# A transformer block on one core: columns of the second modulation begin in the last projection round and are spaced differently around the recurrence; the squares of the keys stand ahead of the block copies

## Chip, core, metric

One NeuronCore of a Trainium2 chip runs the whole program in one launch. The metric is device time in microseconds. The engines are named as in the profile: PE (TensorE matmuls), DVE (VectorE), ACT (ScalarE), POOL (GpSimd) and SP, which does nothing here but issue most of the transfers.

## What is computed

For 256 tokens of width 2048, all in fp32:

```python
mod = silu(c) @ w_ada + b_ada                      # 6 * 2048 values: sh1, sc1, gt1, sh2, sc2, gt2
h = rms_norm(x, norm1_g) * (1 + sc1) + sh1
proj = h @ w_in                                    # RWKV, NSA and merge-gate columns
o_a = rwkv7_mix(...)                               # a gated linear recurrence over the tokens
o_b = nsa_mix(...)                                 # compressed, selected and windowed attention
mixed = sigmoid(mg_a) * (o_a @ w_o_rwkv) + sigmoid(mg_b) * (o_b @ w_o_nsa)
x = x + gt1 * (mixed @ w_out)
h = rms_norm(x, norm2_g) * (1 + sc2) + sh2
x = x + gt2 * (square(relu(h @ w_up)) @ w_down)
```

## The kernel before

**Weights.** Every large weight matrix goes through TensorE in two parts, a rounded high part and a rest. One weight step (`weights`, L221) loads 256 rows by up to 512 columns into a buffer of the pool `raw` (4 buffers), ACT rounds it to `whi`, and DVE subtracts to get `wlo` (both pools have 3 buffers). With the activations split the same way, `mm3` does three matmuls for each block, so a usual step is 24 matmuls of 256 columns (`pp`), in the order (hi, hi), (hi weights, low activations), (low weights, hi activations).

**Columns of the modulation.** `mod` isn't computed on TensorE. Of its 96 columns of 128 values each one is a dot product of 128 rows of `w_ada` with silu(c) on DVE. The short form (`ada`, L173) loads a row block in two halves into the same `raw` pool (tile `ar`, 512 KB each), and each half is one DVE instruction (L158) and a small read of the accumulator. Columns 0 to 31 are needed for the first norm and are computed in the rounds of the first projections, in a longer form with buffers of their own (`ada_long`). Columns 32 to 79 come later, and 80 to 95 in the up projection. `later` is the list of columns still to come, and `next_ada` (L236) is called once in each weight step: it adds `pace[0]` to a counter and, for each whole number, takes one column from the list. So `pace` is columns in one weight step.

**Rounds.** The projections that the recurrence needs run in five rounds over the rows of `w_in` (L384), and within each round over nine groups of columns. The last round takes rows 12 to 15; its last two groups are put into `queue`, with all the other projections (keys, values, merge gates). `fill(n)` (L268) takes n half steps from that queue and is called between the pieces of the recurrence's work, so that TensorE has weight steps to do while a chain of small instructions runs.

**The stretch between.** After the rounds come the preparation of the recurrence (`thl`, `dec`, `kkn`, `AR`, `BK`: elementwise work, much of it on DVE), products within blocks of 32 tokens (`lps` on PE, masked on DVE into `Lm`), a store of `Lm` to DRAM by two transfers that ACT issues (`lsc`, L606), its load in another layout (`em`), a triangular solve in sixty small DVE instructions (`elw`), and then eight chunks of the recurrence (`zps`, `ups`, `hps` on PE with `UV` and `dh` on ACT and DVE; `y` collects the outputs). `yn` is the group norm of the outputs. After it `oa` is made (gate, split), then ACT makes sixteen copies of keys and values into blocks (`kx`, L846), squares two tiles of keys (`ks`, L852), PE sums the squares over heads (`kp`), and a reciprocal root (`krr`, `krp`) is spread by `kb`.

**Order.** Each engine runs its instructions in the order in which they stand in its queue. A scheduler lays that order down when the program is built: it walks the code with its own estimate of durations and takes what is ready and has the best priority. Weight loads, splits and columns carry a better priority (`STREAM`) than the rest. A change of `pace` thus also moves other instructions.

Of the kernel before, what the change touches and what calls it, by code (L numbers as in the profile page):

```python
# [32 lines left out]
def block_kernel(ctx, tc, a):  # L33
# [38 lines left out]
    def T2(name, shape, dt=FT):  # L72
        return t2.tile(shape, dt, name=name, tag="t2")
# [18 lines left out]
    def stt(out, x, s, y, op0, op1):  # L92
        return V.scalar_tensor_tensor(out, x, s, y, op0=op0, op1=op1).ins  # L93
# [174 lines left out]
    def fill(n=1):  # L268

        for _ in range(n):  # L270
            while queue:
                step = next(queue[0], fill)
                if step == "wait":
                    return
                if step is not fill:
                    break
                queue.pop(0)
# [23 lines left out]
    def rsqrt(out, x, scale, ep, tmp):  # L301

        e0 = {0.0: 0, 1e-6: 1, 64e-5: 2}[ep]
        act(out, x, AF.Ln, scale=scale, bias=eps[0:x.shape[0], e0:e0 + 1])
        i = act(out, out, AF.Exp, scale=-0.5)
        tt(tmp, out, out, OP.mult)
        stt(tmp, x, ep / scale, tmp, OP.add, OP.mult)
        stt(tmp, tmp, -0.5 * scale, out, OP.mult, OP.mult)
        stt(out, out, 1.5, tmp, OP.mult, OP.add)
        return i  # L310

    rs = T2("rs", [128, T])
    with tc.issue_after(log_exp([lastt])):
# [70 lines left out]
    for r, (j0, n) in enumerate(rounds):  # L384
        first, last = r == 0, r == len(rounds) - 1
        with prio(START + (1 << 18)):
            stt(am[:, j0:j0 + n], modc[:, 16 + j0:16 + j0 + n], 1.0, prm[:, P_N1 + j0:P_N1 + j0 + n], OP.add, OP.mult)
            lasth = modulate(j0, n, xn)
            if first:
                hold.extend([lasth] * 0 + [None])  # L390
        if not last:
            later.extend(e for j in range(j0 + n, sum(rounds[r + 1])) for e in (j, 16 + j))
            pace[:] = [len(later) / (len(groups) * n // 2 - 1), 0]
        for cols, W, ms, dst, banks in groups:
            g = proj(wseg(cols), W, ms, hhi, hlo, range(j0 // 2, (j0 + n) // 2),
                     dst and acc_evac(dst, first, last), banks, first or banks is None, last or banks is None)
            if last and dst and cols[0][0] >= 3360 and W == 512:
                queue.append(g)
            else:
                run(g)  # L400
        assert not later
    starting[0] = False
    pace[:] = [0.36, 0]


    skv = dr.tile([128, 8, T], FT, name="skv")
# [30 lines left out]
    for c0, dst in ((5968, sma), (8016, smb)):  # L437
        for g in range(4):
            queue.append(proj(wseg([(c0 + g * 512, 512)]), 512, M4, hhi, hlo, range(8),
                              park(lambda b, g=g, dst=dst: dst[:, 4 * g + 2 * b:4 * g + 2 * b + 2])))  # L440
    later.extend(range(32, 80))

    pace[0] = 0.25

    tc.cur_priority = MAIN + (1 << 18)
    pr8, pk8 = prk[:, 0], prk[:, 1]
# [113 lines left out]
    for j in range(8):  # L560
        f = T2("kf", [128, T])
        ts(f, tha[:, j], kah[:, j:j + 1], kam[:, j:j + 1], OP.mult, OP.add)
        tt(pk8[:, j], pk8[:, j], f, OP.mult)
        S.copy(pr8[:, j], shift_mix(pr8[:, j], j))
        fill(1)

    def jc(x):
        return x.rearrange("p j (c s) -> p (j c) s", s=32)
# [142 lines left out]
        rsqrt(st[:, 0], st[:, 1], 1.0 / 64, 64e-5, st[:, 2])  # L711
        tt(y3, y3, st[:, 0][:, :, None].to_broadcast([128, 16, 64]), OP.mult)

    pace[0] = 0.65
    dh = None
    dhs = []
    decv = dec.rearrange("p (j c) -> p j c", c=8)
# [99 lines left out]
    for jp in range(4):  # L817
# [17 lines left out]
        tt(ya, ya, pg.rearrange("p (a t) -> p a t", a=2), OP.mult)  # L835
        split(ya, oa[:, 0, 2 * jp:2 * jp + 2], oa[:, 1, 2 * jp:2 * jp + 2])
        fill(2)
    for kv in range(2):
        for gl in range(2):
            for l2 in range(2):  # L840
# [7 lines left out]
        tt(x3[:, kv], x3[:, kv], pe[:, :, None].to_broadcast([128, 16, 60]), OP.add)  # L848
    ps = PX("kp")
    for b in range(2):  # L850
        sq = T2("ks", [128, 512])
        act(sq, kr[:, 4 + 2 * b:6 + 2 * b].rearrange("p a t -> p (a t)"), AF.Square)  # L852
        head_sums(ps, b, sq)
    r = T2("krr", [64, 512])
    rsqrt(r, ps[0:64], 1.0 / 64, 1e-6, T2("krt", [64, 512]))
    r = parts("krp", r)
# [276 lines left out]
            lastss[0] = mm(ps[:, 0:T], ones, x[:, i], k == 0 and i == 0, k == 1 and i == 1)  # L1133
    rs2 = T2("rs2", [128, T])
    with tc.issue_after(le):
        i = rsqrt(rs2, ps[:, 0:T], 1.0 / D, 1e-6, T2("rst2", [128, T]))
    ahold[:0] = [i, i]
    for q, t in ((0, 0), (0, 1), (1, 0)):
        tokens(q, t)
# [160 lines left out]
```

## Time and profile before

| | |
|---|---|
| Median of three runs | 1647.77 us (1646.96 to 1654.14) |
| Profiled execution | 1648.3 us, span 1646.5 us from first to last instruction |
| PE busy | 1564.2 us, 95% of the span |
| DVE busy | 1149.4 us, 70% |
| ACT busy | 756.3 us, 46% |
| Mean granted TensorE clock | 0.983 of full speed |

Shares are means over stages that differ. The first 200 us are tied to the loads, the last 700 us (up and down projection) keep PE busy all the time, and the stretch that the change touches lies between. "Idle before" in a row is the time that the engine sat before an instruction, and behind the arrow stands what ended it.

### The profile page before, as it was taken

The page shows a single profiled execution, that of the slowest core. Times are in us where ns is not written, and L with a number is a line of the kernel's source. Part 1 is how long each engine was busy: PE and PEld are TensorE (multiplying, and loading weights), DVE is VectorE, ACT ScalarE, POOL GpSimd, SP SyncE. Part 2 cuts the span into 40 slices and gives each one's busy share as a digit, 9 for nine tenths or more (in the row PEclk, how much of TensorE's full clock was granted, in tenths as well). Part 3 has the DMA queues.
Part 4 walks back from the last instruction along what each step waited for, and adds up shares of the span by engine and source line. Part 5 has one row for each costly group of instructions (what it writes and reads, how often), then busy time and mean ns, then how long its engine had stood idle before and what let it go on. Part 6 is the DMA issues. An engine that isn't in the chain of part 4 may idle for free.

```text
span 1646.5 us, 28130 instructions
## 1 busy us (share of the span) xinstructions
PE 1564.2 (95%) x11291; PEld 1380.2 (84%) x11291; DVE 1149.4 (70%) x1695; ACT 756.3 (46%) x1112; POOL 34.9 (2%) x60
## 2 busy tenths in 40 slices
PE   5969999999999889999999899999999999999998
PEld 4968998878889879777899788888888888888886
DVE  7999876977788766777876776666655555555555
ACT  4423358526423365656534444444444544444442
POOL 0000000000000000000000000000000000000001
PEclk9989999998999999999999999999999999999999
DMA  9999767673988777655687477878776555555564
GB/s 371 319 325 342 247 183 236 215 200 120 324 245 276 251 262 258 237 180 167 212 287 269 153 242 239 264 244 260 242 217 189 204 194 193 192 192 194 194 194 148
DMA packets 171174, 381.99 MB, mean 232 GB/s; under 512 B 29249, under 2 KB 43905, under 8 KB 166690
## 3 DMA queue, kind: packets, MB, share of 16 engines
q1 hardware_dynamic: 149344, 355.79, 65.6%
q0 software_dynamic: 4176, 14.17, 2.4%
q10 hardware_dynamic: 17523, 10.24, 2.2%
q8 instruction: 88, 1.44, 0.3%
q14 instruction: 43, 0.35, 0.1%
HBM read 370.13 MB, written 10.01 MB: 231 GB/s over the span
## 4 chain that ended last, share of the span: by engine, by line
PE 48%; DMA 4%; DVE 3%; issue 1%; ACT 1%; DVEq 0%; ACTq 0%
PE pu L99 21%; PE da L99 10%; PE db L99 10%; PE pp L99 5%; DMA ar<-in_w_ada_t 2%; DMA wr<-in_w_out 1%; DVE wlo L90 1%; PE po L99 1%; PE sps L99 1%; DMA gate<-sma 0%; ACT whi L193 0%; PE ptp L1012 0%; DVE ar L158 0%; DVE o L90 0%; ACT p L87 0%
## 5 line engine op out<-in xcount | busy, mean ns | idle before, releaser
L193 ACT CAST whi<-wr 128x1024 fp32r<-128x1024 f32 (+1 forms) x352 | 367.0, 1043 | 513.4 <-PE pp L99 125.6
L90 DVE TENSOR_TENSOR wlo<-wr,whi 128x1024 fp32r<-128x1024 f32 (+1 forms) x352 | 425.8, 1213 | 171.8 <-ACT whi L193 168.7
L99 PE MATMUL pp<-hhi,whi 128*128 128x256 f32 (+1 forms) x1072 | 309.9, 293 | 25.1 <-ACT hhi L87 22.5
L99 PE MATMUL pp<-hlo,whi 128*128 128x256 f32 (+1 forms) x1072 | 307.4, 289 | 0.2 <-DVE hlo L93 0.2
L99 PE MATMUL pp<-hhi,wlo 128*128 128x256 f32 (+1 forms) x1072 | 301.2, 290 | 6.6 <-DVE wlo L90 6.6
L90 DVE TENSOR_TENSOR wdl<-wd,wdh 128x1024 fp32r<-128x1024 f32 x128 | 156.6, 1225 | 170.9 <-ACT wdh L193 170.9
L99 PEld LDWEIGHTS pp<-hhi,whi 128*128 128x128 f32 (+1 forms) x1072 | 209.9, 197 | 33.8 <-ACT hhi L87 23.4
L193 ACT CAST wdh<-wd 128x1024 fp32r<-128x1024 f32 x128 | 134.9, 1055 | 193.7 <-PE db L99 188.6
L99 PEld LDWEIGHTS pp<-hhi,wlo 128*128 128x128 f32 (+1 forms) x1072 | 205.5, 196 | 13.0 <-DVE wlo L90 8.5
L99 PEld LDWEIGHTS pp<-hlo,whi 128*128 128x128 f32 (+1 forms) x1072 | 210.5, 196 | 5.0 <-issue 3.7
L99 PE MATMUL pu<-h2a,whi 128*128 128x512 f32 x512 | 177.2, 398 | 3.1 <-DVE h2a L93 3.1
L99 PE MATMUL pu<-h2b,whi 128*128 128x512 f32 x512 | 179.1, 397 | 0.8 <-DVE h2b L93 0.8
L99 PE MATMUL pu<-h2b,wlo 128*128 128x256 f32 x512 | 140.9, 280 | 0.0
L99 PE MATMUL pu<-h2a,wlo 128*128 128x256 f32 x512 | 135.9, 281 | 0.0
L158 DVE CUSTOM_DVE_ANT_0 ar<-ar,sb,prm 128x1024 f32<-128x1024 f32 x64 | 82.1, 1282 | 73.0 <-DMA ar<-in_w_ada_t 72.9
L99 PEld LDWEIGHTS pu<-h2b,whi 128*128 128x128 f32 x512 | 95.8, 188 | 23.9 <-DVE h2b L93 1.2
L99 PEld LDWEIGHTS pu<-h2a,whi 128*128 128x128 f32 x512 | 95.2, 189 | 24.4 <-DVE h2a L93 3.4
L99 PEld LDWEIGHTS pu<-h2a,wlo 128*128 128x128 f32 x512 | 95.5, 190 | 2.2
L158 DVE CUSTOM_DVE_ANT_0 ar<-ar,sb,adap 128x1024 f32<-128x1024 f32 x64 | 82.0, 1281 | 21.2 <-DMA ar<-in_w_ada_t 20.9
L99 PEld LDWEIGHTS pu<-h2b,wlo 128*128 128x128 f32 x512 | 95.9, 189 | 0.5
L99 PE MATMUL db<-wdh,ul 128*128 128x512 f32 x256 | 79.6, 389 | 0.0
L99 PE MATMUL db<-wdl,uh 128*128 128x512 f32 x256 | 79.6, 389 | 0.0
(342 smaller groups left out, 2676.6 us busy)
## 6 DMA issues: line engine op xcount, KB each, us to landing
wr<-in_w_in SPq DMA_DIRECT2D x136, 512.0 KB, 5.1
ar<-in_w_ada_t SPq DMA_DIRECT2D x128, 512.0 KB, 4.8
wr<-in_w_up SPq DMA_DIRECT2D x128, 512.0 KB, 4.3
wd<-in_w_down SPq DMA_DIRECT2D x128, 512.0 KB, 4.3
ap<-in_w_ada_t SPq DMA_DIRECT2D x32, 1024.0 KB, 6.6
wr<-in_w_out SPq DMA_DIRECT2D x32, 512.0 KB, 5.4
wr<-in_w_in SPq DMA_DIRECT2D x40, 256.0 KB, 3.4
wr<-in_w_o_rwkv SPq DMA_DIRECT2D x16, 512.0 KB, 4.9
```

The lines of the kernel that those rows point to most:

```text
L90: return V.tensor_tensor(out, x, y, op=op).ins
L99: return PE.matmul(out, l, r, start=start, stop=stop, skip_group_check=True).ins
L158: V.tensor_tensor_reduce(out=r, in0=r, in1=s, scale=0.5, scalar=start, op0=OP.mult, op1=OP.add, accum_out=out)
L193: S.copy(hi, raw)
```

## The change

It sets the list of columns 32 to 79 at the head of the last round, with a pace of 0.4 and the short form; before, the list was filled after the rounds and taken at 0.25. It runs at 0.3 from the end of the rounds to the end of the loop that makes `kf` (before 0.25 and, behind `dec`, 0.3), at 0 from there until `Lm` begins (before 0.3), at 0.35 in the recurrence (before 0.65). The pace of 0.12 around `Lm`, and those behind the recurrence, stay. The two squares of keys stand ahead of the sixteen block copies. `rsqrt` returns one value more, which nothing uses.

```diff
         if not last:
             later.extend(e for j in range(j0 + n, sum(rounds[r + 1])) for e in (j, 16 + j))
             pace[:] = [len(later) / (len(groups) * n // 2 - 1), 0]
+        else:
+            later.extend(range(32, 80))
+            starting[0] = False
+            pace[:] = [0.4, 0]
...
-        assert not later
-    starting[0] = False
-    pace[:] = [0.36, 0]
+        assert last or not later
...
-    later.extend(range(32, 80))
-
-    pace[0] = 0.25
+
+    pace[0] = 0.3
...
         fill(1)
 
+    pace[0] = 0
+
     def jc(x):
...
-    pace[0] = 0.65
+    pace[0] = 0.35
     dh = None
...
+    sqk = []
+    for b in range(2):
+        sqk.append(T2("ks", [128, 512]))
+        act(sqk[b], kr[:, 4 + 2 * b:6 + 2 * b].rearrange("p a t -> p (a t)"), AF.Square)
     for kv in range(2):
...
     for b in range(2):
-        sq = T2("ks", [128, 512])
-        act(sq, kr[:, 4 + 2 * b:6 + 2 * b].rearrange("p a t -> p (a t)"), AF.Square)
-        head_sums(ps, b, sq)
+        head_sums(ps, b, sqk[b])
```

Three places in the order of the built programs. The first is DVE's queue in the last round, as a difference (+ new). `ar` with L158 is half a column, the row of `adap` or `modc` behind it reads its accumulator, `wlo` is the low part of a weight step, `pq`, `pl`, `shq` and `twa` belong to the projections and the preparation.

```order
+L90 TENSOR_TENSOR wlo<-wr,whi 128x704
+L158 ISA ar,adap<-ar,sb,prm 128x1024
+L158 ISA adap 128x1
+L90 TENSOR_TENSOR wlo<-wr,whi 128x704
+L158 ISA ar,modc<-ar,sb,adap 128x1024
+L158 ISA modc 128x1
 L90 TENSOR_TENSOR pq<-pq,pp 128x512 x2
 L90 TENSOR_TENSOR wlo<-wr,whi 128x1024 x2
 L90 TENSOR_TENSOR pl<-pl,pp 128x512
+L158 ISA ar,adap<-ar,sb,prm 128x1024
+L158 ISA adap 128x1
 L90 TENSOR_TENSOR pl<-pl,pp 96x256
```

Half columns now stand between the low parts of a round that had none. Counted over the whole queue of DVE, halves of columns 32 and up stand as follows: ahead of `dec` 4 before and 15 now, from there to `knp` (the split ahead of `kkn`) 4 and 4, from `knp` to the last `Lm` 3 and 1, from there to the first `dh` 5 and 6, from there to the last `yn` 38 and 24; by the end of attention the counts are level.

The second place is DVE's queue at the last `Lm`, before and now.

```order
L90 TENSOR_TENSOR wlo<-wr,whi 128x1024 x2
L90 TENSOR_TENSOR Lm<-lps,cs 128x2x256 x3
L158 ISA ar,adap<-ar,sb,prm 128x1024
L158 ISA adap 128x1
L90 TENSOR_TENSOR Lm<-lps,cs 128x2x256
L158 ISA ar,modc<-ar,sb,adap 128x1024
L158 ISA modc 128x1
L90 TENSOR_TENSOR wlo<-wr,whi 128x1024 x5
```

Now:

```order
L90 TENSOR_TENSOR wlo<-wr,whi 128x1024 x2
L90 TENSOR_TENSOR Lm<-lps,cs 128x2x256 x6
L90 TENSOR_TENSOR wlo<-wr,whi 128x1024 x2
L158 ISA ar,adap<-ar,sb,prm 128x1024
L158 ISA adap 128x1
L90 TENSOR_TENSOR wlo<-wr,whi 128x1024
L158 ISA ar,modc<-ar,sb,adap 128x1024
L158 ISA modc 128x1
```

The half column that stood ahead of the last `Lm` now stands behind it and behind two low parts.

The third place is ACT's queue at the block copies, before and now; `oa` is a split of the recurrence's output, `krr` the first step of the keys' root, which reads PE's `kp`.

```order
L193 CAST whi<-wr 128x1024
L193 CAST oa<-ya 128x512
L846 COPY kx<-kx 64x2x15x8 x16
L87 ACTIVATE ks<-kx 128x512 x2
L193 CAST oa<-ya 128x512
L193 CAST whi<-wr 128x1024 x2
```

Now:

```order
L193 CAST whi<-wr 128x1024
L87 ACTIVATE ks<-kx 128x512 x2
L852 COPY kx<-kx 64x2x15x8
L193 CAST oa<-ya 128x512
L852 COPY kx<-kx 64x2x15x8 x13
L193 CAST oa<-ya 128x512
L852 COPY kx<-kx 64x2x15x8 x2
L87 ACTIVATE krr<-kp,eps 64x512
L193 CAST whi<-wr 128x1024 x2
```

The squares lead, and all sixteen copies still stand between one weight conversion and the next, with one `krr` more. On PE, 69 `pp` matmuls stood between the last gate product (`gtp`) and the first `kp`, with 72 `pp` in all before the first that needs a weight tile converted behind the copies; now 19 stand ahead of `kp`, and again 72 ahead of the first that needs such a tile.

## Rows read from the trace of the kernel before

**Rows 1.** Busy time by stretch: length, PE, PEld, DVE, ACT, POOL, clock, DMA share, GB/s.

```profile
200.00:300.00 100.00, 100.00 (x773) 93.70 (x773) 71.22 (x97) 65.75 (x125) 3.41 (x6) 1.00 0.69 209
300.00:355.00 55.00, 51.07 (x513) 43.25 (x512) 51.13 (x90) 21.09 (x31) 1.08 (x2) 1.00 0.61 187
355.00:381.90 26.90, 24.64 (x173) 22.17 (x172) 16.18 (x33) 11.14 (x15) 1.07 (x2) 0.94 0.74 220
...
412.40:560.00 147.60, 139.17 (x1932) 126.05 (x1932) 117.76 (x167) 52.76 (x70) 3.78 (x7) 0.97 0.86 280
...
595.00:606.00 11.00, 6.28 (x18) 2.53 (x17) 7.77 (x9) 9.98 (x19) 1.07 (x2) 0.69 0.28 66
...
800.00:900.00 100.00, 97.31 (x796) 95.64 (x795) 77.79 (x100) 45.74 (x52) 7.15 (x11) 1.00 0.82 281
950.00:1600.00 650.00, 650.00 (x3315) 552.93 (x3315) 381.88 (x422) 285.18 (x337) 1.09 (x2) 1.00 0.67 216
```

**Rows 2.** PE's waits from 300 to 355: total us, times, longest.

```profile
PE psv L99 <- DVE wlo L90: 2.4, 3, 1.5
PE pp L99 <- DVE wlo L90: 1.0, 2, 0.8
```

**Rows 3.** DVE's timeline, 304 to 356: start, us, instruction, idle before.

```profile
305.36 1.29 DVE L158 CUSTOM_DVE_ANT_0 ar<-ar,sb,prm 128x1024 f32<-128x1024 f32 x1 [0.89 <-DMA ar<-in_w_ada_t]
...
312.56 1.28 DVE L158 CUSTOM_DVE_ANT_0 ar<-ar,sb,adap 128x1024 f32<-128x1024 f32 x1
...
348.80 1.88 DVE L90 TENSOR_TENSOR Lm<-lps,cs 128x512 f32<-128x512 f32 x3
352.92 1.28 DVE L158 CUSTOM_DVE_ANT_0 ar<-ar,sb,prm 128x1024 f32<-128x1024 f32 x1 [2.24 <-DMA ar<-in_w_ada_t]
...
354.13 0.69 DVE L90 TENSOR_TENSOR Lm<-lps,cs 128x512 f32<-128x512 f32 x1
```

**Rows 4.** ACT's timeline behind the last `Lm`.

```profile
354.85 3.30 ACTq L606 DMA_DIRECT2D lsc<-Lm  x2
358.26 1.04 ACT L193 CAST whi<-wr 128x1024 fp32r<-128x1024 f32 x1 [11.25 <-PE pp L99]
```

**Rows 5.** PE's timeline in the same place.

```profile
359.36 0.38 PE L99 MATMUL pp<-hhi,whi 128*128 128x256 f32 x1 [1.50 <-ACT whi L193]
360.62 0.58 PE L99 MATMUL pp<-hhi,wlo 128*128 128x256 f32 x1 [0.76 <-DVE wlo L90]
```

**Rows 6.** DVE from 412 to 560 by form: count, busy us, mean ns, idle before.

```profile
L158 DVE CUSTOM_DVE_ANT_0 ar<-ar,sb,adap 128x1024 f32<-128x1024 f32 x20 | 25.6, 1280 | 3.7 <-DMA ar<-in_w_ada_t 3.5
L158 DVE CUSTOM_DVE_ANT_0 ar<-ar,sb,prm 128x1024 f32<-128x1024 f32 x19 | 24.3, 1280 | 8.7 <-DMA ar<-in_w_ada_t 8.7
```

**Rows 7.** PE's waits from 412 to 600: the longest one, which nothing explains.

```profile
PE y L99 <- issue: 4.4, 2, 3.5
```

**Rows 8.** PE's timeline: a head sum at full clock, the last gates, the keys' sums.

```profile
440.93 1.04 PE L99 MATMUL qp<-qs,cs 128*32 128x512 f32 x2
...
585.45 2.08 PE L99 MATMUL gtp<-pl,g 128*128 128x256 f32 x8
600.48 1.91 PE L99 MATMUL kp<-ks,cs 128*32 128x512 f32 x2 [4.72 <-ACT ks L87]
603.26 1.92 PE L99 MATMUL kp<-ks,cs 128*32 128x512 f32 x2
```

**Rows 9.** ACT's timeline around the block copies.

```profile
589.70 1.05 ACT L193 CAST whi<-wr 128x1024 fp32r<-128x1024 f32 x1 [3.40 <-issue]
...
591.17 8.60 ACT L846 COPY kx<-kx 64x240 f32<-64x240 f32 x16
...
601.36 1.99 ACT L193 CAST whi<-wr 128x1024 fp32r<-128x1024 f32 x2
...
605.21 0.68 ACT L87 ACTIVATE krr<-kp,eps 64x512 f32<-64x512 f32 x1 [0.90 <-PE kp L99]
```

**Rows 10.** DVE from 200 to 300 by form: the first halves of columns.

```profile
L158 DVE CUSTOM_DVE_ANT_0 ar<-ar,sb,prm 128x1024 f32<-128x1024 f32 x4 | 5.1, 1283 | 5.8 <-DMA ar<-in_w_ada_t 5.8
```

More of the change, by code (lines that the diff above doesn't have):

```diff
@@ L308, in rsqrt @@
         stt(tmp, tmp, -0.5 * scale, out, OP.mult, OP.mult)
-        stt(out, out, 1.5, tmp, OP.mult, OP.add)
-        return i
+        return i, stt(out, out, 1.5, tmp, OP.mult, OP.add)
     rs = T2("rs", [128, T])
@@ L1135, in block_kernel @@
     with tc.issue_after(le):
-        i = rsqrt(rs2, ps[:, 0:T], 1.0 / D, 1e-6, T2("rst2", [128, T]))
+        i = rsqrt(rs2, ps[:, 0:T], 1.0 / D, 1e-6, T2("rst2", [128, T]))[0]
     ahold[:0] = [i, i]
```

## The prediction

> **What bounds the kernel now.** I began with the table of stretches [rows 1]. From 950 to 1600 us PE is busy for 650.00 of 650 us at a clock of 1.00. No column and no wait counts there, and the change leaves that part's order of work alone. From 200 to 300, the end of the rounds and the first preparation, PE is also busy for 100.00 of 100 us, while DVE is busy for 71.22. The room lies between: from 300 to 355 PE is busy for 51.07 of 55.00 us, from 412.40 to 560 for 139.17 of 147.60, from 595 to 606 for 6.28 of 11.00. In the first of these DVE is busy for 51.13 us, nearly all the time, and PE's waits there, 2.4 and 1.0 us, are waits for DVE's `wlo` [rows 2]. So TensorE sets the end, and the change can only gain what TensorE loses in these stretches, as idle time or at a lower clock. It removes no work: all 96 halves of the 48 columns are still done, and every matmul.
>
> **The preparation and the last `Lm`.** From `knp` to the last `Lm` DVE works without a pause and now has one half column where it had three. Two halves with their waits go: 1.29 and 1.28 us, the wait of 0.89 us for a transfer ahead of one of them [rows 3], 3.5 us in all. PE is idle for 3.93 us in this stretch (55.00 - 51.07) [rows 1], mostly behind DVE. I take 3.0 us as gained and leave 0.9 for waits whose place merely moves; the bounds are 0 and 3.9.
>
> The third half is the one that stands ahead of the last `Lm` in the queue. Three `Lm` are done by 350.7. Then DVE sits for 2.24 us until the half's transfer lands at 352.9, spends 1.28 us on it, and only at 354.13 turns to the last `Lm` [rows 3]. ACT's store `lsc` waits for that. It starts at 354.85, takes 3.30 us to issue, and behind it, at 358.26, comes the next weight conversion [rows 4]. PE has run out by then and waits 1.50 us for `whi` and 0.76 us for `wlo` [rows 5], 2.26 us together. In the new order that half stands behind all the `Lm` rows, so `lsc` can be issued 3.5 us earlier (2.24 + 1.28), more than the wait. But PE's cover shrinks too. Before, 22 value matmuls and 24 `pp` followed the last `lps` without needing a new tile; now only 30 value matmuls do. The streak of lower clock behind that wait (mean 0.94 over 26.90 us from 355 [rows 1], so 26.90 x 0.06 = 1.6 us of lost work) may go or stay. Of 2.26 + 1.6 = 3.9 us I take 1.7, about half; the bounds are 0 and 3.9.
>
> What is late next is the same on both sides: the `elw` chain and ACT's copies for the chunks, whose order hardly changes.
>
> **The recurrence.** DVE handles 39 halves in this stretch, 25.6 + 24.3 us, and sits 3.7 + 8.7 us ahead of them for their transfers [rows 6]. By the order about 14 fewer stand between the first `dh` and the last `yn`, so DVE gets back some 14 x 1.28 = 18 us, and some waits. That is not what TensorE gets back: it has weight steps to do while the chain runs, and it is idle for only 8.43 us (147.60 - 139.17) [rows 1]. Of these 4.4 us are two waits inside `y` that nothing in the trace explains [rows 7]; no column stands there, and I count them as staying. About 4.0 us remain, spread over waits for ACT, for DVE and for weights. I take 1.6. The mean clock of 0.97 [rows 1] stands for 147.60 x 0.03 = 4.4 us, which I leave where they are. Bounds: 0 and 4.0 + 4.4 = 8.4.
>
> **The squares of the keys.** PE waits 4.72 us for `ks` [rows 8], because the squares stand behind sixteen copies that take 8.60 us [rows 9]. It looks like a gain of 4.72. But no weight conversion runs during the copies either: one ends at 590.75, the next starts at 601.36 [rows 9]. PE's cover in between is 72 `pp` behind the last gates, in both orders. From 587.53, the end of the gates, to 595.76, the start of the wait (600.48 - 4.72) [rows 8], it did 69 of them: 8.23 / 69 = 0.119 us each. In the new order 72 x 0.119 = 8.6 us and two pairs of `kp` at the full-clock 1.04 us of a `qp` pair [rows 8] are done by 598.2. The next tile comes no sooner. Between the two conversions still stand the copies, the squares and two splits, and now `krr` as well, 0.68 us [rows 9]: about 602.0 for its start and 603.1 for its end. So PE waits about 4.9 us for `whi` in place of 4.72 for `ks`. What is gained is the time of `kp` behind the wait: before, PE came to the next tile at 603.26 + 1.92 = 605.2 [rows 8], now at 603.1, 2.1 us sooner. The clock takes some of it: a `kp` pair behind the wait took 1.91 and 1.92 us against 1.04 for `qp`, the mark of half clock, and the mean from 595 to 606 is 0.69 [rows 1]. The matmuls that now follow the wait are dense weight steps, and if the half clock lasts as long behind the wait as the rows show it (some 4.7 us, from 600.48 to 605.2), they lose half of it, 2.3 us. I take 0.5 us of gain between these; bounds: 4.7 gained (if the conversion comes earlier for a reason that I don't see) and 0.5 lost.
>
> The Trainium skill (TensorE: Matmul & The Clock Gate, Part 1: The HAM clock gate) says that the throttled state is the default and that activity releases it. By that rule the dense steps pay the full 2.3 us, and the sum below would be about 0.7 us higher; the rows' low clock behind the wait agrees, but whether it costs the new order as much no run shows yet.
>
> **The last round.** By the order 11 halves more stand ahead of `dec` (15 against 4). In the rows DVE spends 1.28 us on such a half and sits ahead of a first half for 5.8 / 4 = 1.45 us [rows 10]. The work alone is 11 x 1.28 = 14 us against an idle 100 - 71.22 = 28.8 us [rows 1]: it fits. The traffic grows by 11 x 0.52 MB over some 80 us, 70 GB/s on top of 209 [rows 1], and the stretch from 800 to 900 runs at 281 with PE idle for 2.7 of 100 us. That stretch is the nearest row for columns between dense weight steps (pace 0.31). I take 0.5 us lost; bounds: 0 and the 12 us of the slow rival.
>
> **Sum.** -3.0 - 1.7 - 1.6 - 0.5 + 0.5 = -6.3 us. Against the profiled execution's own 1648.3 us (1.8 around the span) that gives 1642.0. The median of the runs is 0.5 lower than that execution, so I predict 1641.5. All gains at their bounds would give 3.9 + 3.9 + 8.4 + 4.7 = 20.9 off, about 1627.
>
> **The rivals.**
> - *More comes back.* The waits in `y` and the streaks of low clock in the recurrence go with the columns. For it: the low means stand in just these stretches [rows 1]. Against it: nothing ties them to columns. Taking, beyond my sum, 4.4 of unexplained waits and about 3 of the clock: 1641.5 - 7.4 = 1634.
> - *The columns weren't in the way.* PE has its weight steps, and each wait taken from DVE comes back as another, as at the keys. For it: DVE frees 18 us in the recurrence where PE has 4 us to win. Against it: the wait for the last `Lm` is a plain one, with its cause in the row. 1647, give or take 2.
> - *Slower: the last round starves.* Columns and weights share the four `raw` buffers. DVE takes its queue in order, so a half whose transfer is late holds the `wlo` behind it. If 11 halves come as late as the rows' first halves do, 11 x (1.28 + 1.45) = 30 us no longer fit into 28.8. PE has two tiles ahead, 48 x 0.119 = 5.7 us; from there on each late us is PE's. If the transfers grow later by 1 us in a half, about 12 us are lost, and with the 4.7 us of the first term kept the time is 1648 - 4.7 + 12 = 1655. Against it: DMA share 0.69 and room on DVE. The Trainium skill (Trainium Kernel Development and Optimization, Key Constraints) says that transfers of all queues run on the same 16 DMA engines and interleave; by that the columns slow the weights' transfers there too, and no row of before shows how much.
>
> **How the numbers follow.** What a measurement of this kernel can tell from no change is about 0.5%, 8 us. The forecast, 1638 to 1646, has a chance of 0.45; more comes back 0.22; no gain 0.16; slower 0.17. Faster by over 8 us needs less than 1639.5: the second case and somewhat over a quarter of the first, 0.35. Slower by as much needs more than 1656, about two thirds of the last case, 0.11. The range of 1631 to 1654 leaves out the lower third of the second case and the upper two thirds of the last, under 2 in 10.
>
> **What would show it.** Right: PE's waits for `wlo` from 300 to 355 fall under 1 us; `lsc` follows the last `Lm` without a half column between; `ks` is no longer waited for, and PE waits 4 to 6 us for `whi` in its place; PE stays at 100 from 200 to 300; some 25 halves stand in the recurrence. Wrong: PE idle in the last round, or a wait of the recurrence that grows, since its chunks now come sooner after each other, or a `whi` gap at the copies under 2 us.

## The result, and the profile after

The changed kernel takes 1657.2 us (median of 18 runs, 1651.21 to 1664.2), the kernel before on the same chip 1646.87 us. The ratio is 1.0068, 95% interval 1.0054 to 1.0083: 11.2 us slower by the ratio (10.3 by the medians), where 6.3 faster was forecast. One of the 18 runs of the kernel before took 8531.53 us and is not in the ratio. The profiled execution has a span of 1655.0 us (before 1646.5) and a mean clock of 0.979 (0.983).

First the stretches of [rows 1] for the changed kernel, with the same columns:

```profile
200.00:300.00 100.00, 95.53 (x733) 88.75 (x732) 79.65 (x116) 62.59 (x121) 2.35 (x4) 1.00 0.80 255
300.00:355.00 55.00, 50.27 (x533) 43.87 (x533) 51.07 (x88) 23.28 (x35) 2.17 (x4) 1.00 0.67 192
355.00:381.90 26.90, 24.84 (x164) 21.56 (x163) 17.37 (x34) 9.47 (x10) 1.08 (x2) 1.00 0.76 241
412.40:560.00 147.60, 140.56 (x1930) 125.84 (x1928) 101.31 (x139) 53.19 (x71) 3.79 (x7) 0.97 0.73 233
...
800.00:900.00 100.00, 93.86 (x757) 91.37 (x757) 77.76 (x101) 43.57 (x50) 7.00 (x11) 1.00 0.84 285
950.00:1600.00 650.00, 649.17 (x3325) 552.75 (x3324) 385.35 (x433) 287.95 (x342) 1.09 (x2) 1.00 0.66 216
```

Two stretches that were nearly full are no longer: 200 to 300 us has lost 4.5 us of PE, and 800 to 900 us another 3.4 (97.31 before). Where the forecast saw room, little has come back: 300 to 355 us is 0.8 us worse, and in the recurrence DVE is busy for 16 us less while PE has 1.4 us more. The windows are the same in time and not in work: the first `ups` comes at 417 us in the change and at 412 before.

The last round. PE's waits from 200 to 300 us, where [rows 1] had none:

```profile
PE pvp L99 <- ACT whi L193: 2.8, 1, 2.8
PE pp L99 <- DVE wlo L90: 1.1, 1, 1.1
PE pp L99 <- ACT whi L193: 0.6, 1, 0.6
```

Behind them stands ACT, which waits for its weights. Its conversions in the same 100 us, by form, the kernel before first and the changed one second:

```profile
L193 ACT CAST whi<-wr 128x1024 fp32r<-128x1024 f32 x28 | 29.6, 1056 | 25.5 <-PE pp L99 18.0 <-issue 3.7 <-PE pvp L99 2.0
```

```profile
L193 ACT CAST whi<-wr 128x1024 fp32r<-128x1024 f32 x26 | 27.5, 1057 | 29.0 <-DMA wr<-in_w_in 21.4 <-PE pp L99 5.4 <-DVE wlo L90 2.2
```

Before, ACT waited for PE to free a tile, which is the mark of weights that come early. Now it waits 21.4 us for transfers of weights.

The preparation. PE's waits from 300 to 355 us, then DVE and ACT at the last `Lm`, which answer to [rows 2 to 4]:

```profile
PE pp L99 <- DVE wlo L90: 3.3, 3, 1.4
PE psv L99 <- DVE wlo L90: 1.5, 2, 1.3
```

```profile
347.41 4.08 DVE L90 TENSOR_TENSOR Lm<-lps,cs 128x512 f32<-128x512 f32 x6
354.31 1.23 DVE L90 TENSOR_TENSOR wlo<-wr,whi 128x1024 fp32r<-128x1024 f32 x1 [2.82 <-ACT whi L193]
```

```profile
351.53 1.53 ACTq L608 DMA_DIRECT2D lsc<-Lm  x2
353.23 1.05 ACT L193 CAST whi<-wr 128x1024 fp32r<-128x1024 f32 x1 [7.59 <-PE psv L99]
```

The six `Lm` stand in a row, and the store starts 3.3 us sooner and takes 1.53 us to issue in place of 3.30. But PE's waits for `wlo` are 4.8 us where they were 3.4. The wait behind the store ([rows 5], 2.26 us) is gone, and one of nearly the same size stands some 11 us further on, behind a conversion that waits for its weights (ACT first, then PE):

```profile
370.18 1.04 ACT L193 CAST whi<-wr 128x1024 fp32r<-128x1024 f32 x1 [8.12 <-DMA wr<-in_w_in]
```

```profile
371.28 0.38 PE L99 MATMUL pp<-hhi,whi 128*128 128x256 f32 x1 [1.31 <-ACT whi L193]
...
372.54 0.39 PE L99 MATMUL pp<-hhi,wlo 128*128 128x256 f32 x1 [0.76 <-DVE wlo L90]
```

The recurrence. DVE's halves from 412 to 560 us, for [rows 6], then PE's waits from 412 to 600 us, for [rows 7]:

```profile
L158 DVE CUSTOM_DVE_ANT_0 ar<-ar,sb,adap 128x1024 f32<-128x1024 f32 x14 | 17.9, 1281 | 5.9 <-DMA ar<-in_w_ada_t 5.8
L158 DVE CUSTOM_DVE_ANT_0 ar<-ar,sb,prm 128x1024 f32<-128x1024 f32 x13 | 16.7, 1284 | 27.4 <-DMA ar<-in_w_ada_t 27.4
```

```profile
PE y L99 <- issue: 3.9, 2, 2.4
PE kp L99 <- ACT ks L87: 3.8, 1, 3.8
PE pp L99 <- issue: 2.8, 1, 2.8
PE ups L99 <- DVE UV L90: 1.7, 2, 0.9
PE zps L99 <- DVE dh L90: 1.4, 1, 1.4
```

Twelve halves fewer save DVE 15.3 us of work. It sits 33.3 us ahead of the others, where it sat 12.4. Two waits of PE for the chain, for `UV` and for `dh`, are new: 3.1 us. Two of before are gone, 1.9 us:

```profile
PE y L99 <- ACT UV L743: 1.0, 1, 1.0
PE zps L99 <- DVE yn L90: 0.9, 1, 0.9
```

The keys. ACT around the copies, for [rows 9], and PE's sums, for [rows 8]:

```profile
593.12 1.04 ACT L193 CAST whi<-wr 128x1024 fp32r<-128x1024 f32 x1 [6.68 <-DMA wr<-in_w_in]
594.07 1.15 ACT L87 ACTIVATE ks<-kx 128x512 f32<-128x512 f32 x2
...
596.07 7.08 ACT L852 COPY kx<-kx 64x240 f32<-64x240 f32 x13
...
605.54 1.98 ACT L193 CAST whi<-wr 128x1024 fp32r<-128x1024 f32 x2
```

```profile
594.75 1.91 PE L99 MATMUL kp<-ks,cs 128*32 128x512 f32 x2 [3.78 <-ACT ks L87]
...
606.62 0.39 PE L99 MATMUL pp<-hhi,whi 128*128 128x256 f32 x1 [0.66 <-ACT whi L193]
```

The squares lead, and yet PE waits 3.78 us for them, because they stand behind a conversion that itself waited 6.68 us. The row puts that down to its weights; ACT's own queue was also taken by the issue of another transfer, which ended at 593.03, within 0.1 us of the conversion's start, so the rows don't part the two causes:

```profile
585.85 7.18 ACTq L899 DMA_DIRECT2D w<-in_w1v  x1
```

Before, the same issue ended at 589.66, just ahead of the conversion at 589.70, whose 3.40 us no transfer explains [rows 9]:

```profile
585.27 4.39 ACTq L895 DMA_DIRECT2D w<-in_w1v  x1
```

### The profile page after: what moved, and what is told of

Read it like the earlier page. It is cut to its first block, busy times and chain, and to the rows that moved or that the text cites. A ratio compares the mean times of both kernels' runs of the same rounds, so it can differ in the third digit from the quotient of the medians.

```text
span 1655.0 us, 28133 instructions
## 1 busy us (share of the span) xinstructions
PE 1567.5 (95%) x11291; PEld 1382.3 (84%) x11291; DVE 1148.5 (69%) x1695; ACT 759.1 (46%) x1112; POOL 35.1 (2%) x60
## 4 chain that ended last, share of the span: by engine, by line
PE 66%; DMA 14%; DVE 10%; issue 5%; ACT 3%; ACTq 0%; DVEq 0%; SPq 0%; POOL 0%; POOLq 0%
PE pu L99 21%; PE pp L99 16%; PE da L99 10%; PE db L99 10%; DMA ar<-in_w_ada_t 6%; DMA wr<-in_w_in 4%; DVE wlo L90 4%; DMA wr<-in_w_out 2%; PE pvp L99 2%; ACT whi L193 1%; DVE ap L158 1%; DVE ar L158 1%; DMA ap<-in_w_ada_t 1%; PE po L99 1%; PE sps L99 1%
## 5 line engine op out<-in xcount | busy, mean ns | idle before, releaser
L99 PE MATMUL pp<-hhi,wlo 128*128 128x256 f32 (+1 forms) x1072 | 302.8, 292 | 12.5 <-DVE wlo L90 9.7
L158 DVE CUSTOM_DVE_ANT_0 ar<-ar,sb,prm 128x1024 f32<-128x1024 f32 x64 | 82.2, 1284 | 97.0 <-DMA ar<-in_w_ada_t 96.9
L158 DVE CUSTOM_DVE_ANT_0 ar<-ar,sb,adap 128x1024 f32<-128x1024 f32 x64 | 82.0, 1281 | 21.5 <-DMA ar<-in_w_ada_t 21.3
## 6 DMA issues: line engine op xcount, KB each, us to landing
wr<-in_w_in SPq DMA_DIRECT2D x40, 256.0 KB, 3.6
```

The costliest lines, as they stand in the source:

```text
L99: return PE.matmul(out, l, r, start=start, stop=stop, skip_group_check=True).ins
L158: V.tensor_tensor_reduce(out=r, in0=r, in1=s, scale=0.5, scalar=start, op0=OP.mult, op1=OP.add, accum_out=out)
```

## The experiments

A ratio is to the kernel before on the same chip; 0.001 is 1.65 us. A single kernel's runs lie some 6 us to either side of their median, and two profiles of one order (before, and the squares alone) part by 3.7 us by the time of `fps`. Some profiled executions lie far from their kernel's median (a_jc3 1649.44 us against 1656.6, p4_sq 1639.84 against 1646.96). So kernels are compared by their ratios, and a profile's sums are good to about 4 us at best. Three sums are made of each profile. "Late at `gps`" is the time of the first `gps` less that of before, plus 0.119 us for each weight matmul that the order has done fewer by then (`gps` is an early product of the preparation; the change: 259.0 - 256.0 + 12 x 0.119 = 4.4, and 4.5 from unrounded times). The same difference is taken from the first `ups` to `fps` (the recurrence, up to a small product behind it), and from the last `sps` of attention to `ss`, the merge-gate and output projections. The next column counts halves between 780 and 950 us. The last one adds DVE's waits for halves that have an instruction of the chain (`UV`, `dh`, `yn`, `gst`) next behind them, from the first `ups` to `fps`; other halves in between are passed over. The kernels are told one by one below.

| kernel | ratio | late at gps | ups to fps | sps to ss | halves behind 780 | chain held |
|---|---|---|---|---|---|---|
| before | 1 | 0 | 0 | 0 | 18 | 8.0 |
| the change | 1.0068 | 4.5 | 3.7 | 2.4 | 22 | 6.8 |
| p1_last | 0.9977 | 4.1 | -4.3 | -5.8 | 8 | 4.0 |
| p2_jc0 | 1.0148 | 2.2 | 15.2 | 2.1 | 21 | 19.9 |
| p4_sq | 0.9999 | -0.2 | -2.5 | 2.6 | 18 | 8.5 |
| u1_long | 1.0088 | 1.7 | 7.3 | -0.4 | 22 | 3.6 |
| a_jc3 | 1.0056 | 3.0 | -2.4 | 1.3 | 20 | 11.6 |
| a_rec5 | 1.0079 | 4.1 | 8.0 | -1.4 | 14 | 18.8 |
| u2_rec65 | 1.0019 | 3.5 | 4.9 | -5.5 | 11 | 8.3 |
| p1_sq | 0.9969 | 3.3 | -1.4 | -6.2 | 8 | 1.7 |
| a_no69 | 1.0003 | 4.3 | 9.1 | -8.5 | 2 | 12.1 |
| b_no69 | 0.9962 | -1.2 | 0.0 | -5.6 | 3 | 5.0 |
| a_skip_last | 1.0036 | -0.1 | 9.7 | 3.2 | 21 | 4.9 |
| b_rec10 | 1.0099 | -0.9 | 15.7 | -0.3 | 8 | 6.9 |
| b_skip_rec | 1.0010 | -1.9 | 5.7 | 0.1 | 20 | 8.3 |
| p2_skip_rec | 1.0021 | -0.1 | 0.4 | 1.4 | 22 | 7.2 |
| a_skip_rec | 1.0034 | 2.2 | 1.2 | 4.5 | 20 | 5.1 |
| p1_02 | 1.0027 | 0.7 | 3.8 | 0.4 | 12 | 8.5 |

By the same sum the change is 4.5 us late at `gps`, 4.3 at the first `ups`, 7.9 at `fps`, 4.9 at the last `sps`, 7.3 at `ss` and 8.5 at its end. The stretch from `fps` to the last `sps`, which the table leaves out, gives 3.0 us back.

The last column doesn't follow the loss from `ups` to `fps` over all kernels: b_rec10 loses 15.7 us with 6.9 us held and u1_long 7.3 with 3.6, where a_jc3 has 11.6 us held and loses nothing. In the change it is lower than before (6.8 against 8.0; the text on record for b_skip_rec has 6.8 for before).

**One part of the change alone.** p1_last puts the early start into the kernel before, with the later paces as they were:

```diff
+        else:
+            later.extend(range(32, 80))
+            starting[0] = False
+            pace[:] = [0.4, 0]
...
-        assert not later
-    starting[0] = False
-    pace[:] = [0.36, 0]
+        assert last or not later
...
-    later.extend(range(32, 80))
```

> Before, with the columns begun in the last round at 0.4 and every later pace as before. Theory of the shared buffers (half columns and weight tiles take turns in the four raw buffers, SP issues in that order, so weight tiles land late): PE idle of 4 to 5 us between 200 and 275 us, behind whi that waits for its transfer, and a time 3 to 6 us above before. Rival theory of cover (the loss of the change comes from TensorE's fill work leaving the preparation and the recurrence): no more than 1 us lost ahead of 275 us, time within 2 us of before or a little faster, since the recurrence has as many columns per step as before.

Measured 0.9977 (0.9958 to 0.9997): 4 us faster, though it is 4.1 us late at `gps`. The loss ahead of 275 us is there as the shared buffers had it; the loss of the whole kernel is not.

p2_jc0 puts the pace 0 of the preparation into the kernel before:

```diff
+    pace[0] = 0
+
     def jc(x):
```

> Before, with pace 0 in the preparation alone (from the end of the loop that makes kf to Lm). The prediction's term: the half ahead of the last Lm is gone, lsc starts 3 to 4 us earlier behind the last Lm, the wait of 2.26 us behind it goes, time 2 to 5 us below before. Theory of cover: the chain is shorter, but PE reaches the same places with less fill work and waits there instead (for weights behind the transfers around em and g2), time within 2 us of before.

Measured 1.0148 (1.0123 to 1.0173), 24 us slower by the ratio (the medians part by 21): the largest number of the study, from an edit that moves two halves out of the stretch ahead of the first `dh` and two out of the recurrence, and that the forecast had counted as a gain. Both answers above, a gain and no change, are missed. It loses nothing up to the first `ups` and 15 us from there to `fps`. One place shows how. DVE, ACT and PE from 561 to 577 us:

```profile
565.56 1.28 DVE L158 CUSTOM_DVE_ANT_0 ar<-ar,sb,prm 128x1024 f32<-128x1024 f32 x1 [5.54 <-DMA ar<-in_w_ada_t]
566.78 0.08 DVE L158 DVE_READ_ACCUMULATOR2_ANT adap<- 128x1 f32 x1
566.78 0.68 DVE L90 TENSOR_TENSOR yn<-yn,y 128x512 f32<-128x512 f32 x1
567.49 1.22 DVE L706 TENSOR_REDUCE gst<-yn 128x16 f32<-128x1024 f32 x1
570.45 1.28 DVE L158 CUSTOM_DVE_ANT_0 ar<-ar,sb,adap 128x1024 f32<-128x1024 f32 x1 [1.74 <-DMA ar<-in_w_ada_t]
```

```profile
561.65 0.59 ACT L777 COPY yn<-y 128x512 f32<-128x512 f32 x1 [2.53 <-PE y L99]
...
573.12 0.63 ACT L87 ACTIVATE gsq<-yn 128x512 f32<-128x512 f32 x1 [8.63 <-DVE yn L90]
573.13 0.35 ACTq L794 DMA_DIRECT2D oh<-in_onehot  x1
```

```profile
575.90 1.01 PE L99 MATMUL fps<-oh,rb 32*16 32x256 f32 x2 [6.62 <-DMA oh<-in_onehot]
```

Read from the bottom: PE waits 6.62 us for a small table, whose load ACT issues only behind `gsq`, which waits for `yn`, which stands on DVE behind a half column whose transfer is 5.54 us late, with another 1.74 us behind it. In the kernel before the halves stand ahead of both `yn` there, and the same load is issued at 564.88.

p4_sq has the squares ahead of the copies and nothing else:

```diff
+    sqk = []
+    for b in range(2):
+        sqk.append(T2("ks", [128, 512]))
+        act(sqk[b], kr[:, 4 + 2 * b:6 + 2 * b].rearrange("p a t -> p (a t)"), AF.Square)
...
-        head_sums(ps, b, sq)
+        head_sums(ps, b, sqk[b])
```

> Before, with the squares of the keys ahead of the block copies and nothing else. The prediction's term: PE's wait for ks of 4.7 us turns into a wait of 4 to 6 us for whi (or a shorter one for ks and the rest for whi), time within 1 us of before. Rival: the wait goes, time 4 to 5 us below before.

Measured 0.9999 (0.9981 to 1.0016), as forecast.

u1_long is the changed kernel with the last round's columns in the long form:

```diff
-            starting[0] = False
             pace[:] = [0.4, 0]
...
+    starting[0] = False
```

> The changed kernel, with the columns of the last round in the long form, which has two buffers of its own of 1 MB, in place of halves in the raw pool; the columns, the pace and all that follows as in the changed kernel. Theory of the shared buffers: PE idle in 200 to 275 us falls from 4.5 to under 1.5 us, time 3 to 5 us below the changed kernel (about 1652 to 1654). If it is the traffic itself or DVE's load that makes weights late, PE's idle time there stays at 3 to 5 us and so does the time. Theory of cover: time as the changed kernel within 1.5 us.

Measured 1.0088 (1.0058 to 1.0118): it is only 1.7 us late at `gps`, so the shared buffers have a part in the lateness there, but the whole is no faster. So giving the last round's columns buffers of their own doesn't bring the change's loss back; with 6 runs and another order behind it, a gain of 3 us in one place can't be told apart from a loss in another (7.3 us from `ups` to `fps`).

**Paces one at a time.** From these four the theory of cover got a number: the time follows the count of weight matmuls (`pp`) that the order lays between the first and the last `ups`. It fitted the six kernels known by then, and four more tested it.

```diff
 a_jc3: the change, less
-    pace[0] = 0
 a_rec5: the change, with
-    pace[0] = 0.35
+    pace[0] = 0.5
 u2_rec65: the change, with
-    pace[0] = 0.35
+    pace[0] = 0.65
 p1_sq: p1_last and p4_sq together
```

> The changed kernel with the pace 0 of the preparation taken out (0.3 stays there). Theory cover: the time goes with the number of weight matmuls (pp) that the order lays on TensorE between the first and the last ups of the recurrence. Known so far: 763 gave -4 us against before, 730 (before, and the squares alone) 0, 692 (the change) +11, 682 +14, 670 (pace 0 alone) +21, about 0.3 us for each one that is missing below 730 and 0.12 for each one above. This order has 709, so +6 us (ratio 1.002 to 1.005). Rival zero pace: the loss is that of the pace 0 itself, wherever the order puts the rest, so it all goes, and what is left is the gain of the early start in the last round: -4 us (0.996 to 0.999).

Measured 1.0056 (1.0037 to 1.0074): 2 us better than the change, not 15. In the company of the other edits the pace 0 costs little.

> The changed kernel with a pace of 0.5 in the recurrence in place of 0.35; the pace 0 of the preparation stays. Order: 779 pp between the first and the last ups (the change 692), 33 half columns from the first dh to the last yn (the change 24, before 38). Theory cover: -6 us against before (0.995 to 0.998). Rival zero pace: the pace 0 costs what it costs, +10 us or more (1.006 or more). Rival halves: the time goes with the half columns in the recurrence (24 gave +11, 38 gave 0), so 33 give about +4, and 0.65 less than that.

Measured 1.0079 (1.0052 to 1.0107). Cover, which had 779 matmuls and a gain here, falls.

> The changed kernel with the pace of before, 0.65, in the recurrence. Order: 684 pp between the first and the last ups, 36 half columns from the first dh to the last yn. Theory cover: +14 us against before (1.007 to 1.010), 20 us more than the kernel with 0.5. Rival zero pace: +10 or more as well. Rival halves: +2 (1.000 to 1.002), better than with 0.5.

Measured 1.0019 (0.9998 to 1.0040), where cover had 1.007 to 1.010. The old pace in the recurrence gives 8 us of the 11 back. By its profile that comes behind attention and not in the recurrence: from `sps` to `ss` it stands at -5.5 us where the change has +2.4, with 11 halves left in place of 22, while from `ups` to `fps` it is no better (4.9 against 3.7).

> The kernel before with two parts of the change: columns begun in the last round (0.4), and the squares ahead of the block copies; all later paces as before. Order: 763 pp between the first and the last ups, 65 half columns ahead of the last yn, as in the kernel with the early start alone. Theory cover: as that one, -4 us against before (0.996 to 0.999); the squares add nothing (within 2 us). If the squares gain TensorE's wait for them once the chain is covered, -8 (0.994 to 0.996).

Measured 0.9969 (0.9949 to 0.9988), 1642.89 us: faster than before and the change, and the lowest ratio of a kernel that does all the work, though it can't be told apart from p1_last (0.9977). It parts from the change by the three paces behind the rounds alone, and these cost 1.0068 - 0.9969, 16 us.

**Work left out.** What the old paces do early, the new ones do late. PE from 820 to 900 us is busy for 77.31 of 80 us before, for 73.94 in the change and for 80.00 in p1_sq, with 18, 22 and 8 halves behind 780 us. So a_no69 and b_no69 leave columns 69 to 79 out of the change and of the kernel before:

```diff
+            e = later.pop(0)
+            if 69 <= e < 80:
+                continue
             with prio(STREAM):
-                f(later.pop(0))
+                f(e)
```

> The changed kernel with columns 69 to 79 left out (their values stay 0): these are the 22 half columns that it still does behind 780 us, among the merge-gate and output projections. Theory leftovers: what the recurrence no longer takes is late there, and each half left for that stretch costs TensorE. In the ten profiles so far the time from the last sps to ss, less the weight matmuls done in it at 0.119 us, stands against before at +2.4 us with 22 halves left, 0 with 18, -5.5 with 11 and -6 with 8, some 0.6 us a half. So with none the stretch comes to -7 to -10 against before, and the kernel to about 1646 (ratio 0.998 to 1.002). Rival hidden: TensorE has its weight steps there and columns cost it nothing, the ratio stays at 1.005 to 1.008.

Measured 1.0003 (0.9987 to 1.0020), 10.7 us below the change.

> The kernel before with the same columns 69 to 79 left out (values 0); 18 of these 22 halves stand behind 780 us there. Theory leftovers: the stretch from the last sps to ss loses the same columns, -7 to -10 us, ratio 0.994 to 0.996. What then still parts it from the changed kernel without them (about 7 to 9 us) arises ahead of 780 us. Rival hidden: 0.999 to 1.001, and the two stay 11 us apart.

Measured 0.9962 (0.9941 to 0.9983). The two stretches from 820 to 900 us, a_no69 first:

```profile
820.00:900.00 80.00, 80.00 (x669) 80.00 (x668) 45.48 (x51) 35.44 (x38) 4.28 (x6) 1.00 0.60 207
```

```profile
820.00:900.00 80.00, 80.00 (x669) 80.00 (x668) 42.84 (x46) 32.42 (x36) 4.27 (x6) 1.00 0.61 206
```

From `sps` to `ss` the two kernels stand at -8.5 and -5.6 us, where -7 to -10 was forecast for both. Without columns TensorE is full there from 820 to 900 us, so they are not hidden: columns cost the change 6.06 us of these 80, and before 2.69. The distance of the two kernels falls from 11.2 us to 6.8 (0.0041). That fall, 4.4 us, is uncertain by about 5, so it rests on these rows and on u2_rec65 as much as on the times.

a_skip_last leaves out the columns that the change takes in the last round; the flag is set behind the pace 0.4 and cleared behind the rounds:

```diff
+            e = later.pop(0)
+            if skip[0]:
+                continue
             with prio(STREAM):
-                f(later.pop(0))
+                f(e)
...
             pace[:] = [0.4, 0]
+            skip[0] = True
...
         assert last or not later
+        skip[0] = False
```

> The changed kernel, with the columns left out that are taken in the last round itself (32 to 36, values 0): the early start as before the change, all later columns taken where the change takes them. Theory last round: in six profiles with the early start TensorE comes to the first gps 3.0 to 4.5 us late for the same weight steps (-0.2 to 2.2 without), since a late transfer of a half holds the low part behind it; 1.7 with buffers of their own. So here at most 1.5 late at gps, and 3 to 4 us less in all, 1653 (ratio 1.003 to 1.006). Rival: the lateness is caught up by the end of the preparation, where DVE decides, ratio as the change, 1.006 to 1.008.

Measured 1.0036 (1.0019 to 1.0054), 5.3 us below the change. Its conversions in the last round:

```profile
L194 ACT CAST whi<-wr 128x1024 fp32r<-128x1024 f32 x27 | 28.5, 1055 | 28.9 <-PE pp L99 14.1 <-DMA wr<-in_w_in 8.9 <-issue 3.7
```

It is on time at `gps` (-0.1), and ACT's waits for weights are down from 21.4 to 8.9 us. By its profile, of an execution 4.9 us above its median, it is 2.9 us late again at the first `vps` of the preparation, where the change is 4.0 late: where the 5.3 us come back isn't shown.

b_rec10 asks the opposite of the change, more columns in the recurrence of before:

```diff
-    pace[0] = 0.65
+    pace[0] = 1.0
```

> The kernel before with a pace of 1.0 in the recurrence in place of 0.65: 46 half columns from the first dh to the last yn (before 38), so about ten fewer left behind 780 us, as many left as with the early start at the old paces, without its cost in the last round. Theory leftovers: -5 us (ratio 0.995 to 0.998). The prediction's third term, that columns in the recurrence hold up its chain (14 fewer gain 1.6 us): +1 us or more, at most 5 (1.000 to 1.003). By the number of weight matmuls between the ups (592 against 730), a reading that the kernels with the paces 0.5 and 0.65 have already refuted, it would be +30 or more.

Measured 1.0099 (1.0083 to 1.0114): 16 us slower. The leftovers are down to 8 halves, but the recurrence loses 15.7 us. Both ranges are missed. The prediction's third term has its sign on this side of 0.65 and a size more than ten times too small (1.6 us for 14 halves, and here 8 more). The leftovers miss too: the stretch from `sps` to `ss` gains nothing with 8 halves left (-0.3, where p1_last has -5.8). This order leaves 226 weight matmuls more to be done there than before; whether that is the reason isn't shown, and neither is what holds the recurrence, since its halves wait no longer than before (chain held 6.9 us).

Three more kernels leave out the columns that are taken at the recurrence's pace, with the same flag, and a fourth starts the columns at half the pace:

```diff
 b_skip_rec, p2_skip_rec and a_skip_rec: before, p2_jc0 and the change (0.35), with
     pace[0] = 0.65
+    skip[0] = True
...
     pace[0] = 0.5
+    skip[0] = False
 p1_02: p1_last, with
-            pace[:] = [0.4, 0]
+            pace[:] = [0.2, 0]
```

> The kernel before with the columns left out (values 0) that are taken at the recurrence's own pace; 14 half columns still stand from the first dh to the last yn where there were 38. Theory held chain: DVE takes its queue in order, and a half whose transfer is late holds the chain's instruction behind it (UV, dh, yn, gst). In the profile of before DVE waits 12.5 us for halves from the first ups to fps, 6.8 us of it right ahead of such an instruction; with pace 0 in the preparation it is 24.2 and 19.9 us. So here 3 to 8 us less than before (ratio 0.995 to 0.998). The prediction's third term, 8.4 us at most, gives the same bound.

Measured 1.0010 (0.9992 to 1.0028): a miss. At the old pace and in the old places the recurrence's columns cost nothing that can be seen.

> The kernel before with pace 0 in the preparation, and the same columns of the recurrence left out (values 0). Theory held chain: with the halves the 21 us of the pace 0 go, and it stands within 4 us of the kernel before with the same columns left out (its ratio 0.994 to 1.000). Rival TensorE's order: the pace 0 moved weight matmuls out of the chain (665 pp between the first and the last ups here, 670 with the paces of before), and the loss stays, 10 us or more above that kernel (1.002 or more).

Measured 1.0021 (1.0005 to 1.0038). It stands 1.8 us above b_skip_rec, where p2_jc0 stood 24 above before: the loss of the pace 0 goes with the columns of the recurrence. The count of weight matmuls between the ups doesn't cause it: it is 665 here and 670 in p2_jc0.

> The changed kernel with the columns left out (values 0) that are taken at the recurrence's own pace, 14 halves still from the first dh to the last yn where there were 24. By the sum so far (last round about 5 us, halves left for the stretch behind 780 us about 4.5, little in the recurrence) it stays 6 to 10 us above the kernel before without its columns of the recurrence, ratio 0.999 to 1.004. If the change's loss were in the recurrence, the two would be within 3 us.

Measured 1.0034 (1.0015 to 1.0052), 5.6 us below the change and 4.0 above b_skip_rec: between the two answers. By its profile 4.7 us of the difference to the change are there at the first `ups` already (-0.4 us late against 4.3), where at most four halves are left out, and 2.5 us come from there to `fps`. So the recurrence's part in the change's loss may be small.

> The kernel before with columns begun in the last round at 0.2 in place of 0.4, all later paces as before: 9 halves ahead of dec (14 at 0.4, 4 before), 60 ahead of the last yn (65, 54). Last-round cost about half of the 4 us at 0.4, halves left behind 780 us about 13, so -2 to -6 us against before (0.996 to 0.999), as with 0.4, unless a late half holds the chain, which only the profile shows.

Measured 1.0027 (1.0009 to 1.0045): a miss. Half the early start is not half its gain, it is 4 us slower; PE waits 9.2 us for `wlo` from 200 to 640 us there, and 3.6 us for a `dh`. Why, no run here settles.

## Why the prediction was wrong

- **The last round** is the term that was mis-sized most plainly: 0.5 us, where 4.5 are lost by `gps` and 5.3 go with its columns. (u1_long is only 1.7 us late at `gps` and yet no faster, so 5.3 is not the price of that lateness alone.) The price was taken from the stretch from 800 to 900 us, where PE lost 2.7 of 100 us, as if this were the price of all columns there; and that DVE had room (28.8 us idle) said nothing on when the weights land. The slow rival named late transfers in shared buffers, at over twice the size (12 us) and by another way: it had DVE's `wlo` held behind halves, while PE waits mostly for ACT's `whi` (3.4 of 4.5 us), whose weights land late. The Trainium skill (Trainium Kernel Development and Optimization, Key Constraints) has it that transfers of all queues share the same DMA engines; the trace fits that (DMA share 0.69 to 0.80, ACT's waits for weights from none to 21.4 us), but the sharing isn't the larger part. ACT's waits for weights are 21.4 us in the change, 10.9 with buffers of their own for the same columns (u1_long) and 8.9 without these columns (a_skip_last). So of the 12.5 us that go with the columns, 10.5 go with the shared buffers, by one profile each; what makes the 8.9, where before has none, stays open.
- **The preparation** was to give 3.0 + 1.7 us. The edits did what was written: the halves went, the `Lm` stand in a row, the store starts 3.3 us sooner. The lateness goes only from 4.5 us at `gps` to 4.0 at the first `vps`. The failing step is to take the time of two halves off DVE as time gained on PE ("I take 3.0 us as gained"): PE's waits for `wlo` are 4.8 us where they were 3.4. The wait of 2.26 us behind the store went as forecast, and 2.07 us came back some 11 us later behind late weights; the lower clock of that stretch went (0.94 before, 1.00 now). That is the rival "the columns weren't in the way". Whether the halves alone were worth 3.0 us stays open: in p2_jc0, with the last round as before, 3.4 us come back from `gps` to the first `vps`, but in p4_sq, whose order there is that of before, 1.9 do.
- **The recurrence** was to give 1.6 us, because DVE gets 18 us back. DVE gave them to waits: 33.3 us ahead of halves, before 12.4. Queues are served in order, and a half that waits for its transfer holds what stands behind it, as p2_jc0 shows link by link: `yn`, whose input ACT had copied by 562.24 us, starts at 566.78, right behind the late half. The Trainium skill (PSUM — Partial Sum Buffer, Engine vs sequencer instructions) says that DVE's queue is strictly first in, first out, and these rows agree. In the change one of PE's new waits for the chain follows such rows:

```profile
539.29 1.29 DVE L158 CUSTOM_DVE_ANT_0 ar<-ar,sb,prm 128x1024 f32<-128x1024 f32 x1 [1.30 <-DMA ar<-in_w_ada_t]
...
541.72 1.28 DVE L158 CUSTOM_DVE_ANT_0 ar<-ar,sb,adap 128x1024 f32<-128x1024 f32 x1 [1.13 <-DMA ar<-in_w_ada_t]
...
542.93 1.22 DVE L90 TENSOR_TENSOR wlo<-wr,whi 128x1024 fp32r<-128x1024 f32 x1
544.06 0.68 DVE L90 TENSOR_TENSOR dh<-dh,hps 128x512 f32<-128x512 f32 x1
```

  The first `dh` here is 2.4 us later for two waits of 1.30 and 1.13 us, and `zps` waits 1.42 us for it on PE. So halves are priced by what stands behind them and by whether their data is there, not by 1.28 us each. That is shown for this place and for p2_jc0. For the whole stretch of the change it isn't: PE's waits for the chain there are 1.2 us longer than before (3.1 against 1.9), the change loses 3.7 us from `ups` to `fps`, and its held chain is no longer than before's. The step that failed is "and some waits": with fewer halves DVE's waits ahead of them grew. What makes the rest of the loss there, no run settles.
- **A term is missing**: the columns that the recurrence no longer takes. I had counted halves up to the end of attention and found the counts near each other. In time 22 halves are left behind 780 us where there were 18, and they cost TensorE 6.06 us from 820 to 900 us where it was 2.69. With them left out of both kernels 4.4 us of the distance go, and with the old pace in the recurrence (u2_rec65, 11 left) 8 us. This is the best shown of the parts.
- **The keys** gave what was worked in sum: 0.5 us forecast, nothing measured, since the same copies stand between two conversions. PE's waits around the copies are 4.72 us before, 4.8 in p4_sq, 5.2 in p1_sq and 5.0 in the change. p1_sq waits as forecast (none for `ks`, 3.83 us for `whi`), the change doesn't: 3.78 us for `ks` and 0.66 for `whi`. The step "`ks` is no longer waited for" failed there, by the late conversion ahead of it on ACT, and the `whi` gap under 2 us that was named as a sign of being wrong came. The sum holds whichever of the two is waited for, and 0.5 us can't be told from nothing here.

The parts, 5.3 in the last round, 4.4 left over and 5.6 with the recurrence's columns, make 15.3 us and not 11.2. Each is uncertain by some 4 to 5 us to either side, each kernel with columns left out also has a new order, and the change's own profile has 3.0 us given back from `fps` to the last `sps`. So they show where loss lies and not its exact shares. By edits the account is firmer: early start -4, squares 0, the three paces +16 together. How much of that 16 is the pace 0 depends on the rest of the order: 24 us alone, 2 in the change.

## What to carry to other kernels

Work that fills gaps on an engine with a queue served in order costs what it holds up: look at the instruction behind it, and at whether its transfer will have landed. When a background stream is slowed, find the place where the postponed part ends up and price it there, with that stretch's own rows. Where a scheduler lays the order, try each edit of a pace alone and with the others, since one of them moved the time by 24 us in one order and by 2 in another.

## What the runs showed beyond that

Executions of one kernel differ with the granted clock: the twelve runs of a_jc3 go from 1649.44 us to 1662.6, and the longest three have the clocks 0.973, 0.976 and 0.974 where the shortest three have 0.980, 0.978 and 0.981. That is more than most edits here move, so a single profile can show a mechanism and not its size.
